# Half of the query, key and value projection moved into the attention, modulation on TensorE strips, and norm2 woven between first products

## The chip, the cores and the metric

The kernel runs on one NeuronCore of a Trainium2 chip. The metric is the device time of one execution in microseconds (us). The core has a matrix engine (TensorE, PE in the profile; PEld is its weight load), VectorE (DVE), ScalarE (ACT), GpSimd (POOL), and SyncE (SP), which mostly issues DMAs. Each engine works through its own queue in order.

## What is computed

The reference is one decoder layer on a sequence of 1024 positions, width 1024, in float32:

```python
mod = silu(c) @ ada_w + ada_b                        # six vectors of 1024
sh1, sc1, g1, sh2, sc2, g2 = split(mod, 6)
p = modulate(rmsnorm(x, norm1_g), sh1, sc1) @ w_in   # 1024 x 2048: q, k, v, u of 512 each
o_attn = stick_breaking(rmsnorm(q), rmsnorm(k), v)   # 8 heads of 64
o_ssm = s5(u, ...)                                   # 32 groups of 16 channels
x = x + g1 * (concat(rmsnorm(o_attn), rmsnorm(o_ssm)) @ w_out)
h = modulate(rmsnorm(x, norm2_g), sh2, sc2)
val, gate = split(causal_dwconv(h @ ffn_w_up), 2)    # 2 x 2816 channels
x = x + g2 * ((gelu(gate) * val) @ ffn_w_down)
```

## The kernel before, in words

Matrix products are made of three float32r products each: every operand is split into a rounded part and a rest (`hi`, `lo`), and hi·hi, hi·lo and lo·hi are summed in PSUM. ScalarE makes `hi` (`act_copy`, L160), VectorE or GpSimd the rest (`tt`, L61). Instructions are written out stage by stage, but the build orders each engine's queue by a simulated time line, so work of neighbouring stages is interleaved; `issue_after` and `high_priority` steer it.

The stages are these. **Norm 1 and u** (L152 to L238): for each of eight blocks k of 128 input channels, the shift and scale of the modulation are formed, the normalised x is transposed and modulated into `hhi[k]`, `hlo[k]`, and five of eight tiles of u are accumulated. The modulation vector is c times a 1024 x 256 slice of `ada_w`. For k = 0 it is 16 products with one column (L212). For the others VectorE makes it: a multiplication (L215) and seven multiply-adds (L217) into `ada_acc`, then two one-column products with `ones` sum over the partitions (L220). **State-space parameters** (L240 to L410) are a long string of small VectorE operations. **Query, key projection and state-space batches** (L591 to L625): `proj` (L549) makes 24 matmuls, 512 columns wide, for each of eight row tiles, for queries and for keys; then squares, sums per head (L606), a reciprocal root (`rsqrt`, L71), a scaling (L611), transposes (L615), the split `hl`, and DMAs from the ACT queue to the scratch tensor `qk_d`. Four `ssm_batch` (L429) stand among them. `ada_step` (L587) inserts pieces of `ada_back` (L560), which makes the other modulation vectors, apart from g2, by eight VectorE multiply-adds (L569) on 256 KB loads for each of six pieces of 512. **Values** (L640 to L648) go to `v_d`. 

**Attention** (`head`, L679) runs over eight heads, each in four groups of two query tiles: products z (L697, L698), two sigmoids (L701, L702), a running product on VectorE (the scan, L703), a product on GpSimd (L705), transposes (L710), the split `wh`, `wl` (L714, L715), and products with the values (L720, L721). The loads of the next head are issued with the first tile of the present one (L866). A generator of fillers (`fillers`, L801: the scaling of `w_out`, the statistics of the state-space output, and its half of the output projection) is advanced at fixed points (`marks`, L815), spread from 2% to 87.5% of the attention work. The last head runs its groups in falling order, with the statistics and output projection of finished groups behind them (`tail_stats`, `tail_proj`).

**Norm 2 and first products** (L994 to L1046): `norm2_x`, `norm2_t`, `norm2_s`, `norm2_4` make the operands of the up projection for four groups of 256 positions, the late half (groups 3 and 2) first. The up projection uses one level of Winograd's scheme, seven products of 12 matmuls per channel block m instead of eight, except m = 0, which takes eight direct ones; `first products` of m = 0 and two of m = 1 need only the late half. **Up** (L1128 to L1132): 21 further blocks, with convolution and gating (`conv`, L1090). `g2_rows` (L1051) makes the vector g2 by VectorE multiply-adds during blocks 6 to 9. **Down** (L1150 to L1190): for each half n of the output columns, 22 blocks with 24 matmuls each; the weights are multiplied by g2 on GpSimd (L1160) before they are split.

Of the kernel before, what the change touches and what calls it, by code (L numbers as in the profile page):

```python
# [35 lines left out]
def hybrid_layer_kernel(  # L36
# [53 lines left out]
    cols2_sb = const.tile([128, 194], F32, name="cols2_sb")  # L90
# [3 lines left out]
    gq_sb, gk_sb = cols2_sb[:, 192:193], cols2_sb[:, 193:194]  # L94

# [21 lines left out]
    x1_d = dram.tile([1024, 1024], F32, name="x1_d")  # L117
    x2_d = dram.tile([1024, 1024], F32, name="x2_d")
# [3 lines left out]

    A1 = const.tile([128, 8], F32, name="A1")
# [3 lines left out]
    g1row = const.tile([128, 1024], F32, name="g1row")  # L127
# [4 lines left out]
    hlo = [hp.tile([128, 1024], F32R, name=f"hlo{k}") for k in range(NK)]  # L132
    wp = alloc("w_in")
# [62 lines left out]
    def u_evac(m, hf):  # L196
        uF = wp.tile([128, 8, 64], F32, tag="uF", name="uF", bufs=3)
        act.activation(out=uF, in_=u_ps[m, hf].rearrange("p (c j) -> p j c", j=8), func=AF.Copy)
        sp.dma_start(out=u_d[m * 128:(m + 1) * 128, :, hf * 64:(hf + 1) * 64], in_=uF)

    for k in range(NK):
# [7 lines left out]
        if k == 0:  # L209
            for i in range(2):  # L210
                for r in range(8):
                    pe.matmul(mps[:, i:i + 1], lhsT=raw[:, r, i * 128:(i + 1) * 128], rhs=c_sb[:, r:r + 1], start=(r == 0), stop=(r == 7))  # L212
        else:
            acc = pn.tile([128, 256], F32, tag="ada_acc", name="ada_acc1")
            dve.tensor_scalar(out=acc, in0=raw[:, 0, :], scalar1=c_sb[:, 0:1], scalar2=None, op0=MUL)  # L215
            for r in range(1, 8):
                stt(acc, raw[:, r, :], c_sb[:, r:r + 1], acc, MUL, ADD)  # L217
            for i in range(2):
                cs_ = slice(i * 128, (i + 1) * 128)
                pe.matmul(mps[:, i:i + 1], lhsT=acc[:, cs_], rhs=ones[:, 0:1], start=True, stop=True)  # L220
        tt(dve, S1c[:, k:k + 1], mps[:, 0:1], sh1b[:, k:k + 1], ADD)
        stt(A1[:, k:k + 1], mps[:, 1:2], sc1b[:, k:k + 1], n1g_sb[:, k:k + 1], ADD, MUL)
# [312 lines left out]
    def load_wchunk(cix):  # L535
        his, los = [], []
        for k in range(NK):
            raw = wp.tile([128, 512], F32, tag="wraw", name="w_raw", bufs=4)
            with tc.issue_after(ada_dma[7].ins):
                sp.dma_start(out=raw, in_=w_qkv[cix, k])  # L540
# [241 lines left out]
    def run_all(gen):  # L782
        for _ in gen:
            pass
# [474 lines left out]
```

## Time and profile before

| | before |
|---|---|
| median of 3 runs | 1342.84 us (1341.87 to 1342.91) |
| the profiled execution's own time | 1337.98 us |
| its span, first to last instruction | 1336.2 us |
| PE, DVE, ACT, POOL busy | 1211.5, 1019.7, 594.0, 535.4 us |
| mean granted TensorE clock | 0.95 of full speed |

Busy is the time in which at least one instruction of the engine runs. The granted clock is 1.0 at 2.4 GHz and 0.5 at 1.2 GHz; a stretch between shows a mean of the two. A matmul's row gives its latency, not its pace: successive matmuls overlap, so the pace is the distance between two starts.

### The profile page before, as it was taken

The page shows a single profiled execution, that of the slowest core. Times are in us where ns is not written, and L with a number is a line of the kernel's source. Part 1 is how long each engine was busy: PE and PEld are TensorE (multiplying, and loading weights), DVE is VectorE, ACT ScalarE, POOL GpSimd, SP SyncE. Part 2 cuts the span into 40 slices and gives each one's busy share as a digit, 9 for nine tenths or more (in the row PEclk, how much of TensorE's full clock was granted, in tenths as well). Part 3 has the DMA queues.
Part 4 walks back from the last instruction along what each step waited for, and adds up shares of the span by engine and source line. Part 5 has one row for each costly group of instructions (what it writes and reads, how often), then busy time and mean ns, then how long its engine had stood idle before and what let it go on. Part 6 is the DMA issues. An engine that isn't in the chain of part 4 may idle for free.

```text
span 1336.2 us, 16685 instructions
## 1 busy us (share of the span) xinstructions
PE 1211.5 (91%) x5740; PEld 989.2 (74%) x5740; DVE 1019.7 (76%) x1531; ACT 594.0 (44%) x1006; POOL 535.4 (40%) x415
## 2 busy tenths in 40 slices
PE   5879989999769988679788999999999989999998
PEld 4667768777557776568567888788888878888887
DVE  6999988973887999996799678877777666554552
ACT  5431333331565676535554554445554543222320
POOL 4472451431762446810253553454435334222330
PEclk9989979989679999889889999999999999999999
DMA  8462445557943755041024223322222145447543
GB/s 342 159 143 55 131 136 148 152 152 241 252 111 99 215 175 173 16 142 79 17 87 134 81 88 102 103 95 79 79 93 81 56 157 196 145 145 239 174 142 111
DMA packets 125632, 177.83 MB, mean 133 GB/s; under 512 B 36454, under 2 KB 73958, under 8 KB 124524
## 3 DMA queue, kind: packets, MB, share of 16 engines
q1 hardware_dynamic: 105484, 156.85, 37.7%
q10 hardware_dynamic: 20064, 19.93, 4.5%
q8 instruction: 45, 0.74, 0.2%
q14 instruction: 39, 0.32, 0.1%
HBM read 134.67 MB, written 40.89 MB: 131 GB/s over the span
## 4 chain that ended last, share of the span: by engine, by line
PE 54%; DVE 28%; DMA 8%; issue 4%; ACT 3%; POOL 1%; SPq 1%; DVEq 0%; ACTq 0%; POOLq 0%
PE dnps L1175 6%; PE dnps L1176 6%; PE dnps L1174 6%; PE up_a L982 5%; PE up_a L984 5%; PE up_a L983 5%; DVE ada_acc L67 4%; DVE nb L703 3%; DMA ada_raw<-in_ada_r_dram 3%; PE up_c L982 2%; PE up_c L984 2%; PE up_c L983 2%; PE wops L776 2%; PE wops L777 2%; PE wops L778 2%
## 5 line engine op out<-in xcount | busy, mean ns | idle before, releaser
L61 POOL TENSOR_TENSOR S<-upraw 128x512 f32<-128x512 f32 x42 | 83.4, 1987 | 253.3 <-DVE uplo L61 173.2
L1175 PE MATMUL dnps<-wdlo,ahi 128*128 128x512 f32 x352 | 137.2, 390 | 0.8 <-DVE wdlo L61 0.8
L1174 PE MATMUL dnps<-wdhi,ahi 128*128 128x512 f32 x352 | 134.6, 390 | 3.4 <-ACT wdhi L160 3.4
L1176 PE MATMUL dnps<-wdhi,alo 128*128 128x512 f32 x352 | 137.1, 390 | 0.0
L61 DVE TENSOR_TENSOR uplo<-S,uphi 128x512 fp32r<-128x512 f32 x84 | 96.4, 1151 | 45.4 <-ACT uphi L160 44.2
L61 DVE TENSOR_TENSOR alo<-araw,ahi 128x1024 fp32r<-128x1024 f32 x44 | 61.9, 1407 | 87.7 <-ACT ahi L160 87.7
L61 POOL TENSOR_TENSOR sig<-sig,nb 128x127 f32<-128x127 f32 (+3 forms) x64 | 94.2, 1479 | 84.2 <-DVE nb L703 58.2
L67 DVE SCALAR_TENSOR_TENSOR cv<-up,cols_sb,cv 128x1023 f32<-128x1023 f32 x88 | 116.2, 1322 | 14.3 <-ACT cv L1095 13.2
L61 POOL TENSOR_TENSOR wdraw<-wdraw,g1row 128x512 f32<-128x512 f32 x44 | 69.4, 1581 | 140.7 <-DMA wdraw<-in_w_down_dram 136.3
L703 DVE TENSOR_TENSOR_SCAN nb<-nb 128x128 f32<-128x128 f32 (+3 forms) x64 | 108.4, 1708 | 2.3 <-ACT nb L701 2.0
L160 ACT ACTIVATE ahi<-araw 128x1024 fp32r<-128x1024 f32 x44 | 46.6, 1060 | 141.8 <-PE dnps L1175 119.3
L160 ACT ACTIVATE uphi<-S 128x512 fp32r<-128x512 f32 x84 | 52.7, 631 | 103.6 <-PE up_c L983 30.9
L67 DVE SCALAR_TENSOR_TENSOR ada_acc<-ada_raw,c_sb,ada_acc 128x256 f32<-128x256 f32 (+1 forms) x97 | 73.4, 771 | 25.6 <-DMA ada_raw<-in_ada_r_dram 23.7
L553 PE MATMUL qkvp<-w_hi,hhi 128*128 128x512 f32 x192 | 78.8, 412 | 3.8 <-DVE qssq L606 2.9
L554 PE MATMUL qkvp<-w_lo,hhi 128*128 128x512 f32 x192 | 78.4, 408 | 0.8 <-POOL w_lo L61 0.8
L1174 PEld LDWEIGHTS dnps<-wdhi,ahi 128*128 128x128 f32 x352 | 66.0, 188 | 17.6 <-ACT wdhi L160 3.8
L555 PE MATMUL qkvp<-w_hi,hlo 128*128 128x512 f32 x192 | 77.4, 403 | 0.0
L1175 PEld LDWEIGHTS dnps<-wdlo,ahi 128*128 128x128 f32 x352 | 66.1, 188 | 14.9 <-DVE wdlo L61 1.2
L1176 PEld LDWEIGHTS dnps<-wdhi,alo 128*128 128x128 f32 x352 | 66.1, 188 | 13.5
L160 ACT ACTIVATE uphi<-upraw 128x512 fp32r<-128x512 f32 x67 | 41.8, 629 | 64.5 <-PE up_a L983 26.7
L61 POOL TENSOR_TENSOR cv<-cv 128x1024 f32<-128x1024 f32 x22 | 54.5, 2475 | 34.6 <-ACT cv L1099 34.5
L1095 ACT ACTIVATE cv<-up,cols_sb 128x1024 f32<-128x1024 f32 x44 | 54.7, 1244 | 24.5 <-DVE up L61 23.8
(328 smaller groups left out, 3515.5 us busy)
## 6 DMA issues: line engine op xcount, KB each, us to landing
upraw<-in_w_up_dram SPq DMA_DIRECT2D x88, 256.0 KB, 2.6
araw<-a_d SPq DMA_DIRECT2D x44, 512.0 KB, 3.3
ada_raw<-in_ada_r_dram SPq DMA_DIRECT2D x48, 256.0 KB, 3.1
a_d<-cv ACTq DMA_DIRECT2D x22, 512.0 KB, 2.7
wdraw<-in_w_down_dram SPq DMA_DIRECT2D x44, 256.0 KB, 3.3
ada_raw<-in_ada_a_dram SPq DMA_DIRECT2D x8, 1024.0 KB, 9.4
qk_d<-hl ACTq DMA_DIRECT2D x32, 256.0 KB, 3.0
q<-qk_d SPq DMA_DIRECT2D x32, 256.0 KB, 6.0
```

What stands on the lines that cost most here:

```text
L61: eng.tensor_tensor(out=out, in0=a, in1=b, op=op)
L67: dve.scalar_tensor_tensor(out=out, in0=a, scalar=s, in1=b, op0=op0, op1=op1)
L160: act.activation(out=o, in_=i, func=AF.Copy)
L553: pe.matmul(o, lhsT=lh, rhs=his[k], start=(k == 0), stop=False)
L554: pe.matmul(o, lhsT=lh, rhs=los[k], start=False, stop=False)
L703: dve.tensor_tensor_scan(out=nb[:, 0:n][:, ::-1], data0=nb[:, 0:n][:, ::-1], data1=nb[:, 0:n][:, ::-1], initial=1.0, op0=MUL, op1=ALU.bypass)
L982: pe.matmul(ps, lhsT=hi[:, kt, :], rhs=rh, start=(first and kt == 0), stop=False, skip_group_check=True)
L983: pe.matmul(ps, lhsT=hi[:, kt, :], rhs=rl, start=False, stop=False, skip_group_check=True)
L984: pe.matmul(ps, lhsT=lo[:, kt, :], rhs=rh, start=False, stop=(kt == 3), skip_group_check=True)
L1174: pe.matmul(o[t], lhsT=hi[:, a], rhs=whi, start=(m == 0), stop=False)
L1175: pe.matmul(o[t], lhsT=hi[:, a], rhs=wlo, start=False, stop=False)
L1176: pe.matmul(o[t], lhsT=lo[:, a], rhs=whi, start=False, stop=(m == NM - 1))
```

## The change

- **Strips.** A vector c of 128 partitions is spread to 32 equal columns (`c32`). Each of the eight row blocks of a modulation slice is a float32 product with a stationary operand of 32 columns, written to one of four groups of 32 PSUM partitions (four column strips of the array). The strips hold partial sums; ScalarE copies them, and a product with a constant 1/32 (`mean32`) sums over the partitions. It replaces `ada_acc` in norm 1, in `ada_back` (which now makes g2 too, eight pieces, with two 1 MB loads each into one buffer) and `g2_rows`.
- **Projection in halves.** `load_wchunk` and `proj` take 256 output columns, four heads, at a time. Heads 0 to 3 are projected where all eight were. Heads 4 to 7 are projected by a generator `proj2` during the attention of heads 0 to 3. The fillers of before move to heads 4 to 7 and are placed at 50% to 87.5% of the attention work. At head 4 several pools are released and allocated, and the loads of head 4 are issued there, not during head 3.
- **Norm 2.** Blocks m = 0 and m = 1 both take eight direct products, and these are placed between the steps of norm 2 of groups 1 and 0.
- **Down.** g2 multiplies the output rather than the weights, the first operands are loaded at high priority, and buffers are divided in two pools by the parity of m. Raw up weights use four buffers and two of the attention's.

```diff
+    def strips(ps, raws):
+        for r in range(8):
+            j = r % 4
+            pe.matmul(ps[32 * j:32 * j + 32], lhsT=c32[:, r, :], rhs=raws[r], start=(r < 4), stop=(r >= 4))
...
+        strips(mps[:, 0:256], [raw[:, r, :] for r in range(8)])
+        acc = pn.tile([128, 256], F32, tag="ada_acc", name="ada_acc1")
+        act_copy(acc, mps[:, 0:256])
+        for i in range(2):
+            pe.matmul(mps[:, 256 + i:257 + i], lhsT=acc[:, i * 128:(i + 1) * 128], rhs=mean32[:, 0:1], start=True, stop=True)
...
+    def qk_pair(pl, nh, ps_o, ps_t, cix, hh, tq, w):
+        qk = pl.tile([128, 2, 4, 64], F32, tag="qk", name="qk", bufs=2)
...
+        for j in range(2):
+            proj(o[:, j * 256:(j + 1) * 256], tq * 2 + j, w)
+            if j == 0:
+                yield
+        qf = qk.rearrange("p j h d -> p (j h d)")
+        act.activation(out=qf, in_=o, func=AF.Copy)
+        act.activation(out=o, in_=o, func=AF.Square)
+        dve.tensor_reduce(out=ssq, in_=o.rearrange("p (h d) -> p h d", d=64), op=ADD, axis=AX.X)
+        yield
+        ts(dve, ssq, ssq, 1.0 / HD, EPS, MUL, ADD)
+        rsqrt(small, inv, ssq, 8)
+        yield
...
     def ada_back(ix):
...
+        for hf in range(2):
+            raw = stg.tile([128, 4, 512], F32, tag="adaq", name="ada_raw", bufs=1)
+            sp.dma_start(out=raw, in_=ada_r[ix, :, hf * 4:hf * 4 + 4])
+            if hf == 0:
+                yield
+            for i in range(4):
+                pe.matmul(ps[32 * i:32 * i + 32], lhsT=c32[:, hf * 4 + i, :], rhs=raw[:, i, :], start=(hf == 0), stop=(hf == 1))
+            if hf == 0:
+                yield
...
-    marks = [a + (b - a) * j / n for a, b, n in ((0.02, 0.14, 22), (0.14, 0.80, 24), (0.80, 0.875, 12)) for j in range(n)]
+    marks = [a + (b - a) * j / n for a, b, n in ((0.005, 0.46, 43), (0.50, 0.58, 22), (0.58, 0.82, 24), (0.82, 0.875, 12)) for j in range(n)]
...
+    def proj2():
+        for cix in range(3):
+            w = load_wchunk(pj, cix, 1, 4, 2)
+            yield
+            for tq in range(4):
+                if cix < 2:
+                    yield from qk_pair(pj, 1, psB_new, psB_new, cix, 1, tq, w)
+                else:
+                    yield from v_pair(pj, 1, psB_new, 1, tq, w)
...
+        if hd == NH // 2:
+            run_all(fill)
+            ap_.release()
+            pj.release()
+            hp.release()
...
+            fill = fillers()
+            stk = (head_load_qk(hd), head_load_v(hd))
...
     norm2_t(1, norm2_x(1))
-    norm2_s(1)
+    first_late(0, ("V", "a", 2), ("V", "b"), ("V", "a", 2), ("N", "b"))
+    up_early(1, ("A21", "A22"))
     with tc.high_priority():
         xn0 = norm2_x(0)
...
+    norm2_s(1)
     norm2_4(1)
     norm2_t(0, xn0)
+    first_late(1, ("N", "c"), ("V", "b"), ("N", "b"), ("V", "b"))
...
+    first_early(0)
     norm2_s(0)
+    first_early(1)
     norm2_4(0)
...
-        tt(pool, raw, raw, g2row[:, ns], MUL)
...
-            tt(dve, res, o[t], res, ADD)
+            t_ = dx.tile([128, 512], F32, tag="tmp", name="tmp", bufs=2)
+            tt(dve, t_, o[t], g2row[:, ns], MUL)
+            tt(dve, res, t_, res, ADD)
```

## Rows read from the trace of the kernel before

**Rows 1.** By stage: stretch, length, busy PE, PEld, DVE, ACT, POOL, clock, DMA, GB/s

```profile
0.00:337.00 337.00, 290.12 (x1472) 233.79 (x1472) 281.49 (x654) 113.50 (x184) 132.24 (x127) 0.93 0.56 165
337.00:443.00 106.00, 83.07 (x421) 66.53 (x422) 90.99 (x111) 65.80 (x141) 57.78 (x55) 0.80 0.58 160
443.00:577.00 134.00, 110.64 (x664) 92.73 (x663) 124.65 (x147) 86.81 (x203) 77.16 (x82) 0.93 0.45 137
577.00:650.00 73.00, 68.12 (x315) 55.76 (x314) 51.41 (x145) 35.35 (x66) 3.38 (x2) 0.97 0.29 101
650.00:680.00 30.00, 16.14 (x57) 10.75 (x56) 26.85 (x43) 16.25 (x32) 14.98 (x4) 0.72 0.05 18
680.00:1075.00 395.00, 390.28 (x1707) 320.90 (x1706) 308.97 (x324) 199.15 (x287) 175.45 (x101) 1.00 0.27 92
```

**Rows 2.** VectorE's groups from 0 to 337 us: count, busy, mean ns, idle before

```profile
L67 DVE SCALAR_TENSOR_TENSOR ada_acc<-ada_raw,c_sb,ada_acc 128x256 f32<-128x256 f32 (+1 forms) x97 | 73.4, 771 | 25.6 <-DMA ada_raw<-in_ada_r_dram 23.7 <-DMA o_d<-gt 1.8
...
L61 DVE TENSOR_TENSOR qk<-qk,qinv 128x512 f32<-128x512 f32 x16 | 12.4, 811 | 0.2
...
L606 DVE TENSOR_REDUCE qssq<-qkvp 128x8 f32<-128x512 f32 x16 | 10.8, 681 | 0.0
...
L67 DVE SCALAR_TENSOR_TENSOR rs_h<-qinv 128x16 f32<-128x16 f32 x24 | 8.7, 370 | 0.2
...
L67 DVE SCALAR_TENSOR_TENSOR hl<-qkT,gqk,hl 128x512 fp32r<-128x512 f32 x8 | 6.0, 748 | 3.0 <-ACT hl L618 3.0
```

**Rows 3.** TensorE in order of time: start us, us, at 512 columns

```profile
1149.95 0.39 PE L1174 MATMUL dnps<-wdhi,ahi 128*128 128x512 f32 x1
1150.18 0.39 PE L1175 MATMUL dnps<-wdlo,ahi 128*128 128x512 f32 x1
```

**Rows 4.** The same view at 256 columns, in the attention

```profile
480.23 0.28 PE L721 MATMUL ops<-wl,vsb 128*128 128x256 f32 x1
480.35 0.28 PE L720 MATMUL ops<-wh,vsb 128*128 128x256 f32 x1
```

**Rows 5.** The same view, float32 products, whole array

```profile
202.72 1.50 PE L524 MATMUL gps<-ys,G 128*128 128x128 f32 x12
204.06 1.02 PE L573 MATMUL adps<-ada_acc,ones 128*128 128x512 f32 x2
204.92 0.27 PE L615 MATMUL qkT<-ident,qk 128*128 128x128 f32 x1
```

**Rows 6.** The same view, float32 products on two column halves in turn

```profile
106.39 2.15 PE L490 MATMUL vps<-U,W 128*64 128x128 f32 x32
108.47 0.50 PE L553 MATMUL qkvp<-w_hi,hhi 128*128 128x512 f32 x1
```

**Rows 7.** DMA issues: count, size, us from issue to landing

```profile
ada_raw<-in_ada_a_dram SPq DMA_DIRECT2D x8, 1024.0 KB, 9.4
vsb<-v_d SPq DMA_DIRECT2D x8, 512.0 KB, 5.2
```

**Rows 8.** VectorE in order of time: two scans of 640 columns

```profile
521.13 1.48 DVE L703 TENSOR_TENSOR_SCAN nb<-nb 128x640 f32<-128x640 f32 x1
...
546.47 3.18 DVE L703 TENSOR_TENSOR_SCAN nb<-nb 128x640 f32<-128x640 f32 x1
```

**Rows 9.** GpSimd in order of time, beside the second scan

```profile
546.31 2.00 POOL L61 TENSOR_TENSOR sig<-sig,nb 128x1023 f32<-128x1023 f32 x1
```

**Rows 10.** TensorE's waits from 650 to 680 us: total, times, longest

```profile
PE tp L938 <- ACT h2f L939: 8.0, 5, 3.4
PE up_a L982 <- ACT uphi L160: 5.6, 1, 5.6
```

**Rows 11.** TensorE's waits from 680 to 1110 us

```profile
PE up_a L982 <- DVE up L61: 3.6, 3, 2.0
PE dnps L1174 <- ACT wdhi L160: 3.4, 1, 3.4
```

**Rows 12.** VectorE's groups from 680 to 860 us

```profile
L67 DVE SCALAR_TENSOR_TENSOR g2acc<-g2raw,c_sb,g2acc 128x256 f32<-128x256 f32 x28 | 22.4, 801 | 8.2 <-DMA g2raw<-in_ada_r_dram 8.0
```

More of the change, by code (lines that the diff above doesn't have):

```diff
@@ L208, in hybrid_layer_kernel @@
         mps = psU.tile([128, 512], F32, tag="mps", name="mps", bufs=1)
[L209 to L222, printed above, removed]
+        strips(mps[:, 0:256], [raw[:, r, :] for r in range(8)])
[3 more added lines that the diff above has]
+            pe.matmul(mps[:, 256 + i:257 + i], lhsT=acc[:, i * 128:(i + 1) * 128], rhs=mean32[:, 0:1], start=True, stop=True)
+        tt(dve, S1c[:, k:k + 1], mps[:, 256:257], sh1b[:, k:k + 1], ADD)
+        stt(A1[:, k:k + 1], mps[:, 257:258], sc1b[:, k:k + 1], n1g_sb[:, k:k + 1], ADD, MUL)
         hi = wp.tile([128, 512], F32R, tag="whi", name="wu_hi", bufs=8)
@@ L558, in hybrid_layer_kernel, with run_all @@
+    vlast = [None]
+    def run_all(gen):
+        for _ in gen:
+            pass
     TB, ZB, MB = 3, 2, 2
@@ L572, in ada_back @@
-        if kind == 0:
-            pe.matmul(ps, lhsT=ones, rhs=acc, start=True, stop=True)
-            act.activation(out=g1row[:, o:o + 512], in_=ps, func=AF.Copy)
+        if kind == 0:
+            row = g1row[:, o:o + 512]
+            sp.dma_start(out=row, in_=ada_br[ix:ix + 1, :].to_broadcast([128, 512]))
+        elif kind == 3:
+            row = wp.tile([128, 512], F32, tag="uF", name="g2", bufs=2)[0:1, :]
+            sp.dma_start(out=row, in_=ada_br[ix:ix + 1, :])
+        ps = psA.tile([128, 512], F32, tag="aux", name="adps")
@@ L575, in ada_back @@
+        act_copy(acc, ps)
+        yield
+        ps = psA.tile([128, 512], F32, tag="aux", name="adps")
+        if kind in (0, 3):
+            pe.matmul(ps, lhsT=mean32, rhs=acc, start=True, stop=True)
+            tt(dve, row, ps[0:row.shape[0]], row, ADD)
+            if kind == 3:
+                sp.dma_start(out=g2_d[ix - 6:ix - 5, :], in_=row)
         else:
             for j in range(4):
-                pe.matmul(ps[:, j:j + 1], lhsT=acc[:, j * 128:(j + 1) * 128], rhs=ones[:, 0:1], start=True, stop=True)
+                pe.matmul(ps[:, j:j + 1], lhsT=acc[:, j * 128:(j + 1) * 128], rhs=mean32[:, 0:1], start=True, stop=True)
@@ L626, in hybrid_layer_kernel @@
+            g = qk_pair(stg, 2, psA_o, psA_t, cix, 0, tq, w)
+            for _ in range(2):
+                ada_step(2)
+                next(g)
+            run_all(g)
     smb.release()
     sm.release()
-    xq = alloc("qkraw", side="right")
-    us = alloc("ffnmix", side="right")
     qp = alloc("qk", side="right")
-    xs = alloc("ossm", side="right")
+    op_ = alloc("oatt", side="right")
+    oT = op_.tile([128, NPAIR, 1024], F32, tag="oT", name="oT", bufs=1)
     def head_load_qk(hd):
@@ L1001, in hybrid_layer_kernel @@
     wo.release()
-    op_.release()
     xs.release()
```

304 lines of the change are left out of this document (148 added, 156 removed).

## The prediction, made before the changed kernel was run

> **What bounds the kernel now.** I read the busy time by stage first, then each stage's own groups and waits. The table shows three kinds of stage. Up to 337 us, where the first product of the attention starts, VectorE is busy for 281.5 of 337 us and TensorE for 290.1 at a mean clock of 0.93: both are near full, and VectorE has the added idle time [rows 1]. In the attention, 337 to 577 us, VectorE leads clearly: 91.0 of 106 us and 124.7 of 134, together 215.6 of 240, or 90%, while TensorE has 83.1 and 110.6 at clocks of 0.80 and 0.93 [rows 1]. From 680 us on TensorE is full (390.3 of 395 at clock 1.00), so nothing but less TensorE work or fewer stalls helps there. Between lies a hole: from 650 to 680 us TensorE is busy for 16.1 of 30 us at a clock of 0.72 [rows 1]. So the change takes VectorE work out of the first stage, puts TensorE work into a stage that VectorE bounds, and fills the hole.
>
> **The first stage (0 to 337 us).** VectorE loses the multiply-adds of the modulation: 97 of 0.77 us, 73.4 us busy, and with them a wait of 23.7 us for their loads [rows 2]. Seven opening multiplications go too; at the same length they are some 4 us. Half of the per-head work goes to the attention: of 16 scalings (0.811), 16 sums (0.681) and 16 splits (about 0.75) [rows 2] half is 18 us. The strings of small operations stay as many, since eight pairs of tiles remain. What comes (four row additions, some of a few columns) I set at 4 us. VectorE falls from 281.5 to about 190.
>
> TensorE: the pace is 0.23 us for 512 columns [rows 3] and 0.12 for 256 [rows 4]. The projection had 3 x 8 x 24 = 576 matmuls of the first kind, 131 us, and keeps 576 of the second, 69 us: 62 less. The strips add. A float32 product appears as two records; for 512 columns the two take 204.92 - 204.06 = 0.86 us [rows 5], so 0.43 for 256. On two halves of the array 32 records of 128 columns take 108.47 - 106.39 = 2.08 us, 0.065 each [rows 6], against (204.06 - 202.72)/12 = 0.112 on the whole array [rows 5]: two strips do overlap. Bounds for four products on four strips: one after the other 4 x 0.86 = 3.44 us, all together 0.86. I take all together, since two already run at 1.7 times the pace. In the 2.08 us the 16 pairs at 0.112 would take 1.8, so entering and leaving the strips costs up to 0.3 us; I charge 0.5. Then 16 groups of the six old and two new pieces cost 16 x 1.36 = 22 us, and eight blocks of norm 1, two rounds of 0.43 each, 8 x 1.36 = 11. The one-column products and the sums over partitions I set equal before and after. TensorE's busy time becomes 290 - 62 + 33 = 261.
>
> The Trainium skill, in "TensorEngine Tiling (Array Packing)", section Key Properties, says that changing the tiling mode drains TensorE; that speaks against 24 groups of strips between full-width matmuls. By that rule the sum would hold a drain twice per group, and the trace agrees that it is small: the 0.3 us above is all that rows 5 and 6 leave for it.
>
> VectorE's 190 us, with today's idle time less the 23.7, 337 - 281.5 - 23.7 = 32, end at 222. TensorE can't start before its first 1 MB load, 9.4 us [rows 7], so I let it start at 11: without a gap it ends at 272 with today's clock, at 261 x 0.93 + 11 = 254 with the clock at 1. If it keeps today's idle time (337 - 290 = 47 us) it ends at 308. I take 256, nearest to the full clock, since the groups that make it wait are VectorE's, and those shrink: the attention starts **81 us earlier**, between 29 and 115.
>
> A wait is added: `ada_back` has one buffer, so each of 16 loads of 1 MB starts when the last strips have read it, and behind a strip that waits stands every later matmul. Loads of this size landed in 9.4 us in the crowded first 50 us [rows 7]; one half of a pair's projection, 24 x 0.12 = 2.9 us, surely covers part of it. The queue order is simulated, so I assume projections are put in front of the strips, and price a failure as a rival.
>
> **The attention (337 to 577 us).** No instruction of the heads goes away. Added for heads 4 to 7: 576 matmuls of 0.12 us, 69 us, all beside heads 0 to 3; on VectorE eight pairs with a scaling, a sum, a split, 2.2 us, and a dozen small operations between 0.17 and 0.37 us [rows 2], 2 to 4.4 us, and four value splits: 36 to 55, I take 43. ScalarE gets copies of like number, and its queue 16 DMA issues; it was busy for 65.8 of 106 us [rows 1]. GpSimd gets 12 splits of the weights. A scan of 640 columns took 1.48 us alone and 3.18 beside a 2.00 us GpSimd product [rows 8, 9], so each of them may hold a scan up by about its own length, half of 2.00: up to 12 us, I take 5. VectorE then has 215.6 + 43 + 5 = 264 us, and at today's 90% this is 293.
>
> The Trainium skill, in "SBUF — State Buffer", section Who interferes with whom, says that a VectorE instruction with two SBUF inputs and a GpSimd instruction that reads SBUF exclude each other in full. By that alone the 12 us, not 5, would stand in the sum; the pair of scans agrees with full exclusion, but which meet is a matter of timing.
>
> At head 4 the loads of keys and values are no longer a head ahead; the value load lands in 5.2 us [rows 7], the keys and queries before it, and I charge 10 us for that start. So 303, **63 us longer**, between 40 (93% busy, no bubble) and 100 (heads 0 to 3, with three engines near full, at 75%). Heads 4 to 7 also get denser, as all old fillers are now theirs; that is within the sum, since the work is the same.
>
> **Norm 2 (577 to 680 us).** TensorE's hole is 13.9 us idle, of which 8.0 waits for ScalarE's transposed rows and 5.6 for operands after GpSimd's sums [rows 10], plus 16.1 x 0.28 = 4.5 us for the slow clock [rows 1]. The eight direct products give 11 us of matmuls between the steps, and m = 1 no longer waits for GpSimd. But it takes an eighth product, 12 x 0.23 = 2.7 us. **13 us shorter**, between 0 and 16; next late would be VectorE with 26.9 of 30 us.
>
> **Up and down.** VectorE loses 22.4 us of g2 and its wait of 8.0 [rows 12], which TensorE feels only through waits of 3.6 us [rows 11]: 3 shorter. The first down operands are loaded early: 3.4 us of waiting [rows 11], 3 shorter. GpSimd's weight product cost nothing, hidden by full TensorE. The last output tile has one VectorE operation more, as long as a 512-column scaling, about 0.7. Together **5 shorter**, between 0 and 8.
>
> **Sum.** -81 + 63 - 13 - 5 = -36 us against the profiled 1337.98, or 1302. The median of the runs lies 4.9 us above the profiled execution; I shift by that: 1342.8 - 36 = 1306.8, say **1307**. Its own range is 1280 to 1332.
>
> **Rivals.** *Strips stall on their loads (slower).* The queue puts the strips so that a 1 MB load is covered by only one half projection. For: one buffer, and VectorE already waited 23.7 us for loads of a quarter of this size [rows 2]. Against: those waits came mostly from three small buffers in turn. With landings of 6 us, between the 5.2 for half the size and the 9.4 of the crowd [rows 7], each costs 3.1, 16 make 50: 1357. It decides from 36/16 = 2.3 us per load. *The attention takes it all back.* Heads 0 to 3 have 69 us more TensorE and 43 more VectorE work; if they and the start of head 4 take the upper bound of 100, the time is 1344, no change. For: clock 0.80 and all engines rising together; against: in the stretch from 443 us VectorE was already busy for 93% beside the same fillers. *The strips do not overlap fully.* Two at a time adds 16 x 0.86 + 8 x 0.86 = 21 us: 1328; one at a time adds 62 us, 1369. Rows 6 speak against the latter; nothing shows four. *More than forecast.* The first stage ends at VectorE's bound of 222 and the attention takes 290: 34 + 13 less, 1260.
>
> **Chances.** Forecast 0.60, stalled loads 0.12, attention takes all 0.13, strips 0.10 (mostly two at a time), more 0.05. About 0.2% is what a measurement of this kernel can tell from no change. Slower: the stalls, half of the second rival and a little of the strips, 0.20; same: a part of the second, 0.05; faster 0.75. The range 1270 to 1350 leaves out the stalled loads and the best case, under 2 in 10.
>
> **What would show it.** The attention's first product near 256 us, with VectorE at about 190 us busy before it. No DMA named as releaser of strips for more than 2 us each. Groups of four strips 1 to 1.4 us apart, start to next full-width start. Heads 0 to 3 in 135 to 155 us with TensorE over 85% busy; VectorE some 264 us busy in the whole attention. Head 4 starting within 10 us of its loads. No stretch of 30 us with a clock under 0.9 between the attention and the up products. The forecast is wrong if the attention grows by more than the first stage shrinks, or if TensorE's waits before it name ada_raw.

## The result, and the profile after

The changed kernel takes 1490.49 us, median of 4 runs (1489.31 to 1491.63), against 1342.36 for the kernel before (4 runs, 1340.33 to 1342.91): a ratio of 1.1107, 95% interval 1.1087 to 1.1126. It is 148 us slower; I had forecast 36 us faster. The profiled execution after took 1491.63 us with a span of 1489.8, 153.6 more than the span before.

Four marks split both spans: the first product of the attention (z), the end of its last product with the values, the first down product, the end.

| stage | before, us | after, us | difference | forecast |
|---|---|---|---|---|
| up to the first z | 337.2 | 370.6 | +33.4 | -81 |
| attention | 241.7 | 368.6 | +126.9 | +63 |
| norm 2 and up | 512.7 | 506.4 | -6.3 | -13 and some of -5 |
| down | 244.6 | 244.2 | -0.4 | the rest of -5 |

The page of the changed kernel, parts 1 (busy time) and 6 (DMA issues, with us to landing):

```profile
PE 1281.8 (86%) x6552; PEld 1049.6 (70%) x6552; DVE 956.6 (64%) x1508; ACT 597.5 (40%) x1015; POOL 462.7 (31%) x362
...
ada_raw<-in_ada_r_dram SPq DMA_DIRECT2D x16, 1024.0 KB, 5.1
```

Its stages, with the columns of [rows 1]; they answer to those rows:

```profile
0.00:222.00 222.00, 186.77 (x1300) 156.30 (x1300) 152.12 (x467) 81.00 (x135) 86.66 (x89) 0.95 0.50 160
222.00:371.00 149.00, 81.05 (x374) 52.54 (x373) 32.22 (x64) 16.09 (x21) 15.79 (x19) 0.57 0.43 120
371.00:572.00 201.00, 154.86 (x1042) 139.66 (x1041) 122.16 (x220) 86.88 (x199) 69.94 (x75) 0.87 0.31 87
572.00:739.00 167.00, 128.43 (x650) 104.92 (x649) 131.04 (x164) 86.22 (x182) 75.24 (x73) 0.83 0.44 142
739.00:811.00 72.00, 58.74 (x252) 45.40 (x252) 46.42 (x132) 31.43 (x59) 8.87 (x5) 0.88 0.36 124
811.00:842.00 31.00, 28.95 (x126) 22.69 (x125) 27.56 (x48) 20.52 (x38) 0.00 (x0) 0.89 0.01 1
842.00:1240.00 398.00, 397.74 (x1738) 325.57 (x1737) 336.63 (x293) 203.89 (x293) 203.27 (x101) 1.00 0.24 81
```

VectorE lost the work that the change took from it: 152.1 + 32.2 = 184 us are busy before the attention, against 281.5 [rows 1]. The time did not follow. From 222 to 371 us no engine is full: TensorE is busy 81 of 149 us at a clock of 0.57, VectorE 32. In heads 0 to 3 (371 to 572 us; 123 us before) and 4 to 7 (572 to 739; 118 before) no engine is full either: VectorE is busy for 61% and 78% of them, where it had 90% [rows 1]. The hole of [rows 1] in norm 2, 16.1 of 30 us, is filled: 28.95 of 31 us.

**What the third row of the table hides.** The stage holds the end of the output projection, and that grew: from the last product with the values to the last projection product it is 54.8 us before (578.9 to 633.7) and 67.8 after (739.2 to 807.0), for nearly the same products. From there to the end of the span it is 702.5 before and 682.7 after, 19.8 shorter. TensorE's waits from 739 to 842 us, projection first, then what is left of the 8.0 and 5.6 us of [rows 10]:

```profile
PE wops L824 <- POOL wohi L177: 8.6, 2, 4.8
PE wops L825 <- POOL wolo L61: 2.6, 3, 1.2
...
PE tp L1011 <- ACT h2f L1012: 0.8, 1, 0.8
PE up_a L1055 <- ACT T1hi L174: 0.7, 1, 0.7
```

Three of the four weight tiles that this projection reads are split by GpSimd only now (737.6 to 757.8 us), one after another through one buffer; in the kernel before the last was under way at 578.7. In order of time, one of them:

```profile
741.11 3.43 DMA woraw<-in_w_out_dram
744.64 1.30 DVE woraw L67
...
746.01 1.05 POOL wohi L177
...
747.14 2.36 POOL wolo L61
```

**What fills 222 to 371 us.** First TensorE's waits there (total, times, longest), then the chain of waits that ends at the attention (start, us, what):

```profile
PE adps L640 <- DMA ada_raw<-in_ada_r_dram: 44.1, 9, 9.7
PE yps L522 <- DVE S L61: 7.8, 2, 5.7
```

```profile
322.20 1.91 PE adps L640 x8
...
324.13 5.01 DMA ada_raw<-in_ada_r_dram
...
329.18 1.58 PE adps L640 x8
...
341.02 7.74 DMA k<-qk_d
...
348.83 10.98 DMA ada_raw<-in_ada_r_dram
...
359.94 1.97 PE adps L640 x8
...
361.93 4.89 DMA ada_raw<-in_ada_r_dram
...
366.87 1.98 PE adps L640 x8
```

The loads land in 5.1 us by the page, sooner than those of [rows 7], and still it reads as strips, load, strips, load: with one buffer a load starts when the strips before it have run, and the next strips wait for it. As written, the code has a `yield` behind the first load of each piece but none between the second load and its strips, and all projections made ahead of the attention had ended at 227 us: ten of the 16 groups of strips came later, with only products of the state-space batches in front. One load was issued behind the key load in SP's queue and took 10.98 us. That queue stops as well: from 222 to 371 us it waits 32.0 us for strips to free the buffer, with loads of the batches and heads behind; no run separates this from TensorE's waits.

**The strips themselves** overlap as forecast. In order of time a group of four 512-column products (eight records) goes from 199.14 to 200.13 us, start to next full-width start, 0.99 us at full clock; one product on the whole array took 0.86 [rows 5]. Six of the 16 groups ran so; the ten behind 227 us took 1.6 to 1.9 us each, all but one wholly at half the clock. The row of TensorE's groups from 96 to 372 us (count, busy, mean ns, idle before) adds up to 25.4 us for all 16, where I had 22: a pace better than forecast and a clock that I had not forecast happen to give nearly that sum.

```profile
198.93 0.28 PE L564 MATMUL vp<-w_hi,hlo 128*128 128x256 f32 x1
199.14 1.06 PE L640 MATMUL adps<-ada_raw,c 128*32 128x512 f32 x8
200.13 0.38 PE L562 MATMUL vp<-w_hi,hhi 128*128 128x256 f32 x1
200.36 0.28 PE L563 MATMUL vp<-w_lo,hhi 128*128 128x256 f32 x1
```

```profile
L640 PE MATMUL adps<-ada_raw,c 128*32 128x512 f32 x128 | 25.4, 877 | 44.4 <-DMA ada_raw<-in_ada_r_dram 44.4
```

The Trainium skill, "TensorEngine Tiling (Array Packing)", section Key Properties, says that changing the tiling mode drains TensorE. The trace leaves room for it: 0.13 us in the group (0.99 - 0.86), 0.09 in front (0.21 from 198.93 to 199.14, against the pace of 0.12 [rows 4]) and 0.11 behind (0.23 from 200.13 to 200.36), together 0.33 us, near the 0.3 that the prediction allowed.

### The profile page after: what moved, and what is told of

It reads as the page before. It is cut to its first block, busy times and chain, and to the rows that moved or that the text cites. A ratio compares the mean times of both kernels' runs of the same rounds, so it can differ in the third digit from the quotient of the medians.

```text
span 1489.8 us, 18144 instructions
## 1 busy us (share of the span) xinstructions
PE 1281.8 (86%) x6552; PEld 1049.6 (70%) x6552; DVE 956.6 (64%) x1508; ACT 597.5 (40%) x1015; POOL 462.7 (31%) x362
## 3 DMA queue, kind: packets, MB, share of 16 engines
q1 hardware_dynamic: 100488, 157.38, 33.4%
## 4 chain that ended last, share of the span: by engine, by line
PE 66%; DVE 14%; DMA 9%; ACT 4%; POOL 3%; issue 2%; SPq 1%; ACTq 0%; DVEq 0%; POOLq 0%
PE dnps L1233 5%; PE dnps L1232 5%; PE dnps L1231 5%; PE up_a L1056 5%; PE up_a L1057 5%; PE up_a L1055 5%; DVE nb L751 3%; DMA ada_raw<-in_ada_r_dram 3%; PE up_c L1056 3%; PE up_c L1057 3%; PE up_c L1055 3%; PE qkp L563 2%; PE qkp L562 2%; PE qkp L564 2%; PE wops L824 2%
## 5 line engine op out<-in xcount | busy, mean ns | idle before, releaser
L67 DVE SCALAR_TENSOR_TENSOR cv<-up,cols_sb,cv 128x1023 f32<-128x1023 f32 x88 | 144.0, 1639 | 20.9 <-ACT cv L1157 18.8
L61 DVE TENSOR_TENSOR alo<-araw,ahi 128x1024 fp32r<-128x1024 f32 x44 | 55.5, 1262 | 122.5 <-ACT ahi L174 120.0
L61 POOL TENSOR_TENSOR S<-upraw 128x512 f32<-128x512 f32 x40 | 76.3, 1909 | 180.5 <-DVE uplo L61 89.7
L751 DVE TENSOR_TENSOR_SCAN nb<-nb 128x128 f32<-128x128 f32 (+3 forms) x64 | 99.7, 1571 | 3.4 <-ACT nb L749 3.2
L174 ACT ACTIVATE uphi<-S 128x512 fp32r<-128x512 f32 x80 | 49.8, 624 | 84.3 <-POOL S L61 67.8
L563 PE MATMUL qkp<-w_lo,hhi 128*128 128x256 f32 x256 | 76.6, 299 | 3.2 <-POOL w_lo L61 3.2
L562 PE MATMUL qkp<-w_hi,hhi 128*128 128x256 f32 x256 | 77.5, 303 | 0.0
L564 PE MATMUL qkp<-w_hi,hlo 128*128 128x256 f32 x256 | 76.5, 299 | 0.0
L61 DVE TENSOR_TENSOR uplo<-upraw,uphi 128x512 fp32r<-128x512 f32 x68 | 70.4, 1037 | 2.0 <-ACT uphi L174 1.9
L174 ACT ACTIVATE uphi<-upraw 128x512 fp32r<-128x512 f32 x68 | 42.9, 631 | 67.5 <-POOL cv L61 31.2
L824 PE MATMUL wops<-wohi,ohi 128*128 128x512 f32 x128 | 54.3, 431 | 13.4 <-POOL wohi L177 9.3
L768 PE MATMUL ops<-wh,vsb 128*128 128x256 f32 x160 | 51.0, 339 | 16.7 <-DVE oT L61 7.1
```

Source lines behind the costliest of these rows:

```text
L61: eng.tensor_tensor(out=out, in0=a, in1=b, op=op)
L67: dve.scalar_tensor_tensor(out=out, in0=a, scalar=s, in1=b, op0=op0, op1=op1)
L174: act.activation(out=o, in_=i, func=AF.Copy)
L562: pe.matmul(o, lhsT=lh, rhs=wh, start=(k == 0), stop=False)
L563: pe.matmul(o, lhsT=lh, rhs=wl, start=False, stop=False)
L751: dve.tensor_tensor_scan(out=nb[:, 0:n][:, ::-1], data0=nb[:, 0:n][:, ::-1], data1=nb[:, 0:n][:, ::-1], initial=1.0, op0=MUL, op1=ALU.bypass)
```

## Experiments

Kernels with one time ran once. The single runs of the kernel before spread over 1335 to 1346 us, so from one run a difference under some 10 us is not read without its trace.

### The second modulation: left out, put back on VectorE, moved, loaded in halves

**e1_no_back** leaves the second modulation's loads, strips and sums out (g1, sh2, sc2 and g2 are constants).

```diff
-    ada_gen = (q for ix in range(8) for q in ada_back(ix))
...
+    ada_gen = iter(())
```

> The changed kernel without its 16 loads of 1 MB, their strips and their sums (g1, sh2, sc2 and g2 are constants; the strips of norm 1 stay). Theory: after 222 us, when all projections are done, strips that wait for single-buffered 1 MB loads stand in TensorE's queue ahead of the last two state-space batches and of the attention; the chain of waits names these loads for about 75 us there. Without them the first product of the attention falls from 370.6 us to 285 to 300, the time to about 1405 to 1420. Rival: the four state-space batches, a serial chain through single buffers, bound the stage now that the projections no longer run beside them at a high clock; then the start falls by under 35 us, to 335 or later, and the time stays above 1455.

1378.76 us, 112 less than the changed kernel, more than expected; first z at 266.5 us. The state-space batches, which end at 321.0 in the changed kernel, end at 244.6. The rest of the stage:

```profile
222.00:266.00 44.00, 24.83 (x201) 22.11 (x200) 15.12 (x29) 12.68 (x17) 12.81 (x16) 0.82 0.59 157
```

So the batches did not bound the stage; they stood behind the second modulation's loads and strips. Without it the stage ends 71 us earlier than before; the forecast had 81, and that with 22 us of strips in it.

**e9_back_on_vector** puts only the second modulation back on VectorE.

```diff
-            raw = stg.tile([128, 4, 512], F32, tag="adaq", name="ada_raw", bufs=1)
-            sp.dma_start(out=raw, in_=ada_r[ix, :, hf * 4:hf * 4 + 4])
...
-                pe.matmul(ps[32 * i:32 * i + 32], lhsT=c32[:, hf * 4 + i, :], rhs=raw[:, i, :], start=(hf == 0), stop=(hf == 1))
...
+            raw = stg.tile([128, 512], F32, tag="adaq", name="ada_raw", bufs=3)
+            sp.dma_start(out=raw, in_=ada_r[ix, :, r])
...
+                stt(acc, raw, c_sb[:, r:r + 1], acc, MUL, ADD)
...
-                ada_step(2)
+                ada_step(4)
```

> The changed kernel with the second modulation alone put back on VectorE, as before the change (256 KB loads, three buffers in turn, one multiply-add per load; four pieces ahead of each half pair): everything else of the change stays. Theory that strips in TensorE's queue stop it at each load, while VectorE has time to wait: first product of the attention at 275 to 315 us instead of 371, attention and rest as in the changed kernel, time 1395 to 1435. Rival (the loads or the state-space batches bound the stage on whichever engine): first product at 340 to 370, time 1460 to 1490.

1434.78 us, 56 less; first z at 312.8. The theory holds, at the upper end. Against no second modulation at all (266.5) it costs 46 us on VectorE and 104 on strips. The same work costs over twice as much of this stage on strips, with these loads, as on VectorE.

**e7_early** asks for the strips earlier.

```diff
-                ada_step(2)
+                ada_step(4)
```

> The changed kernel with the strips of the second modulation asked for twice as often (four pieces instead of two ahead of each half pair of queries and keys), so that they end beside the first state-space batches and not behind the last. Theory that it is the place in the order that costs (loads between the late state-space batches, and an uncovered tail): first product of the attention at 290 to 320 us instead of 371, time 1410 to 1445. Rival (16 waits for a single-buffered load cost their 5 us in TensorE's queue wherever they stand): first product at 345 to 375, time 1465 to 1500.

1499.62 us, first z at 383.9: slower still. The strips end at 330.7 instead of 371.6, but the last state-space batch ends at 363.4 instead of 321.0, and TensorE has 79.9 of 162 us, at half the clock:

```profile
222.00:384.00 162.00, 79.88 (x349) 52.23 (x349) 34.51 (x64) 17.53 (x23) 21.86 (x25) 0.53 0.37 106
```

The theory that the place in the order costs falls: asked for earlier, the same loads delayed the state-space batches instead.

**e8_halves** keeps order and memory, with two 512 KB buffers and two loads ahead.

```diff
+        raw = stg.tile([128, 2, 512], F32, tag="adaq", name="ada_raw", bufs=2)
...
-            raw = stg.tile([128, 4, 512], F32, tag="adaq", name="ada_raw", bufs=1)
...
+            if n + 2 < 32:
+                ada_load(n + 2)
```

> The changed kernel with the same 1 MB of space as two buffers of 512 KB, each load issued as soon as its buffer is read, two ahead of the strips, at the same places in the order. Theory that the single buffer costs (a load starts only when the last strips have run, and TensorE's queue waits for all of it): first product of the attention at 300 to 330 us instead of 371, time 1420 to 1450. Rival (the loads stand behind others in SP's queue, and the state-space batches behind them): within 15 us of 371, time 1475 to 1495.

1470.0 us, first z at 354.3: between the two. TensorE's waits from 222 to 354 us fall from 44.1 to 23.0 us, and the start of the attention moves by 16:

```profile
PE adps L649 <- DMA ada_raw<-in_ada_r_dram: 23.0, 14, 6.3
```

So the single buffer is at least 16 of the 104 us that the second modulation costs on strips (e1), and neither theory holds in full: the chain of waits still goes from load to strips to load, six times 4.3 to 5.7 us and once 7.4. Two buffers of 1 MB were not tried.

### The three parts alone, in the kernel before

**e4_strips_norm1**: strips in norm 1 only.

```diff
-            dve.tensor_scalar(out=acc, in0=raw[:, 0, :], scalar1=c_sb[:, 0:1], scalar2=None, op0=MUL)
-            for r in range(1, 8):
-                stt(acc, raw[:, r, :], c_sb[:, r:r + 1], acc, MUL, ADD)
...
+        strips(mps[:, 0:256], [raw[:, r, :] for r in range(8)])
...
+        act_copy(acc, mps[:, 0:256])
```

> The kernel before with the strips in norm 1 alone. If the strips do what was forecast (four at once, about 1 us a group), VectorE loses some 30 us of multiply-adds before the state-space parameters, these end near 76 us instead of 101, and with a first stage bounded by VectorE the attention starts 15 to 25 us earlier: 1318 to 1328. Rival: the stage is bounded by the chain of four state-space batches and TensorE behind it; the earlier start is still passed on whole, but a part is lost where the projections are now late: 1328 to 1340. If the strips cost more than they save: above 1343.

1336.25 us, 5 runs (ratio 0.9951, 0.9929 to 0.9973), in the rival's range. The longest part of the state-space parameters ends at 71.2 instead of 101.0 us, but the first z stands at 340.9 against 337.2: of 30 us gained none reaches the attention, since TensorE was already busy for 214 of 233 us from 104 us on. The gain is 5 us by the timed runs; the two profiled spans differ by only 1.1 us, so I can't place it in a stage.

**e5_norm2_alone**: norm 2 between eight first products.

```diff
-    RAWS, OPS = 6, 7
+    RAWS, OPS, FIRST = 4, 8, 2
...
+    first_late(1, ("N", "c"), ("V", "b"), ("N", "b"), ("V", "b"))
...
+    first_early(0)
...
+    first_early(1)
```

> The kernel before with the third part of the change alone (norm 2 between eight first products of output blocks 0 and 1; g2 and the down operands as before). Forecast's step: 13 us shorter between the end of the attention and the full up products. The changed kernel showed 513 -> 506 us from the last output product of the attention to the first product of the last phase, so 4 to 10 us: a time of 1332 to 1338. Rival (the hole is refilled by another wait, VectorE's own 27 of 30 us): 1340 to 1343. If norm 2 costs: above 1345.

1335.07 us, 10 runs (0.996, 0.9936 to 0.9984). As expected, and half of the 13 us forecast. The hole is filled:

```profile
652.00:683.00 31.00, 29.32 (x137) 23.93 (x136) 27.48 (x44) 21.58 (x37) 8.66 (x4) 1.00 0.09 30
```

It still lasts 31 us, with VectorE at 27.5, and from the last product with the values to the first down product it is 506.1 us instead of 512.7. The waits of [rows 10] are gone, but others came. From the last projection product to the first down products, TensorE's waits of 22.6 us before add up to 15.4 here; the largest:

```profile
PE up_a L982 <- ACT up L160: 3.9, 3, 2.3
PE dnps L1180 <- ACT wdhi L160: 3.4, 1, 3.4
PE dnps L1181 <- DVE wdlo L61: 2.3, 1, 2.3
PE adps L1075 <- DVE g2acc L67: 2.3, 1, 2.3
```

In the changed kernel, where g2 is off VectorE here and the down operands come early, they add up to 2.3.

**e6_strips_small_norm2**: norm 1 and the second modulation on strips, each product on its own 256 KB load, three buffers; norm 2 as in e5. All heads are projected before the attention.

```diff
             raw = wp.tile([128, 512], F32, tag="uF", name="ada_raw", bufs=3)
             sp.dma_start(out=raw, in_=ada_r[ix, :, r])
-            stt(acc, raw, c_sb[:, r:r + 1], acc, MUL, ADD)
             yield
+            j = r % 4
+            pe.matmul(ps[32 * j:32 * j + 32], lhsT=c32[:, r, :], rhs=raw, start=(r < 4), stop=(r >= 4))
```

> The kernel before (all eight heads projected before the attention) with norm 1 and the second modulation on four strips, the second modulation's loads kept small (256 KB each, three buffers in turn), and norm 2 between first products. If strips and norm 2 are sound and only the large single-buffered loads and the moved projections cost: VectorE loses some 60 us before the attention but TensorE stays full there, so 10 to 20 us shorter in all, 1320 to 1335. Rival (strips at this place make TensorE wait for each 256 KB load, 48 of them): first product of the attention later than 345 us, time over 1345.

1356.14 us, 4 runs (1.011, 1.0077 to 1.0143), first z at 363.1: the rival. Its cause is only partly the waits, 13.2 us. TensorE's groups from 96 to 363 us:

```profile
L577 PE MATMUL adps<-ada_raw,c 128*32 128x512 f32 x96 | 41.7, 680 | 13.2 <-DMA ada_raw<-in_ada_r_dram 13.2
```

48 products, one per load, take 41.7 us, 0.87 each, as long as a whole-array product; in the changed kernel 64 in groups of four take 25.4. From its start to the next full-width start one product alone takes 0.98 us, about as long as a group of four:

```profile
188.16 1.05 PE L577 MATMUL adps<-ada_raw,c 128*32 128x512 f32 x2
189.14 0.50 PE L559 MATMUL qkvp<-w_lo,hhi 128*128 128x512 f32 x1
```

In e8, two together take 0.98 as well (198.75 to 199.73 us). So in this kernel the time goes per group, and the strips gain only where several stand together, for which their operands must be there at once.

**e11_strips_norm2**: the two gains, the edits of e4 and e5, together.

```diff
+        strips(mps[:, 0:256], [raw[:, r, :] for r in range(8)])
...
+    RAWS, OPS, FIRST = 4, 8, 2
```

> The kernel before with the two parts of the change that were faster by themselves: norm 1's modulation on strips, and norm 2 between first products; second modulation on VectorE and all eight heads projected before the attention, as before. If the two gains add (0.9951 and 0.996): ratio 0.989 to 0.993, 1327 to 1333 us, ahead of both kernels. Rival (norm 1's gain is only a shift that the wait for the projections takes back): 0.994 to 0.998.

1327.18 us, 6 runs (0.9902, 0.987 to 0.9935): the gains add. It is 1% ahead of the kernel before and far ahead of the changed one, with the second modulation on VectorE and all heads projected at their old place.

### Heads 0 to 3: the pairs

**e2_proj2_first** runs the projection of heads 4 to 7 to its end ahead of head 0's work.

```diff
-    fill = proj2()
+    run_all(proj2())
+    fill = iter(())
```

> The changed kernel with the projection of heads 4 to 7 run before head 0 instead of beside heads 0 to 3; nothing is left out. Theory: beside the heads it is a serial string (one pair every 20 us, of which 10 to 13 are a dozen small VectorE operations queued between scans), still unfinished when head 3 ends, and head 4 waits for all of it. Alone, a pair needs 13 us, as the last three did after head 3: about 8 x 13 + 4 x 6 + 10 = 140 us before head 0, then heads 0 to 3 take 75 to 90 us without it; first product of the attention to head 4 near 85, and the time within 25 us of the changed kernel, 1470 to 1515. Rival: heads 0 to 3 are long because engines are full; then they still take over 120 us without the filler, and the time is above 1540.

1511.45 us. The build put head 0's products beside the first pairs. With little else beside them (VectorE is busy for 61 of 169 us from 362 us on) the twelve pairs still take 156 us, 362.5 to 518.7. Heads 1 to 3 then take 66 us, 22 each, so full engines, the rival, are not what holds them. TensorE names the scaling in each of the eight query and key pairs:

```profile
PE qkT L588 <- DVE qk L61: 40.3, 8, 7.3
```

So a pair is a string: products, copy, sum, a dozen small VectorE operations, scaling, transposes; the next pair's products stand behind the transposes in TensorE's queue. **In the changed kernel** scans and splits of the heads come between its links. VectorE in order of time, from a pair's sum to its scaling:

```profile
400.26 0.69 DVE L578 TENSOR_REDUCE qssq<-qkp 128x8 f32<-128x512 f32 x1 [4.50 <-ACT qkp L577]
...
403.66 0.14 DVE L67 SCALAR_TENSOR_TENSOR rs_h<-qinv 128x8 f32<-128x8 f32 x1
403.72 1.22 DVE L751 TENSOR_TENSOR_SCAN nb<-nb 128x512 f32<-128x512 f32 x1
404.85 0.77 DVE L61 TENSOR_TENSOR rs_h<-rs_h,qssq 128x8 f32<-128x8 f32 x1
...
407.74 1.49 DVE L751 TENSOR_TENSOR_SCAN nb<-nb 128x640 f32<-128x640 f32 x1
...
409.53 1.17 DVE L61 TENSOR_TENSOR rs_h<-rs_h,qssq 128x8 f32<-128x8 f32 x1
...
411.16 0.67 DVE L61 TENSOR_TENSOR qk<-qk,qinv 128x512 f32<-128x512 f32 x1
```

10.9 us pass from the start of the sum to that of the scaling, for small operations that last 3.9 us per pair (31.2 us in all from 371 to 572 us, over eight). Over the eight pairs it is 9.6 us on average.

**e3_short_string** leaves out the three correction steps of the reciprocal root for heads 4 to 7 (the first estimate is used).

```diff
-        rsqrt(small, inv, ssq, 8)
+        rsqrt(small, inv, ssq, 8, 3 if hh == 0 else 0)
```

> The changed kernel with the reciprocal root of heads 4 to 7 cut from eleven small VectorE operations to two (its three Newton steps are left out there, so these heads are scaled roughly). It takes 8 x 9 operations of 0.17 us, 12 us of VectorE time, away. Theory of the serial string: each pair beside the heads loses 6 to 10 us of its 20, head 4 starts 35 to 65 us earlier than 201 us after the first product, and the time falls by 35 to 65 us, to 1425 to 1455. Rival (full engines): no more than the 12 us of work go, 1478 or later.

1446.99 us, 43.5 less. From sum to scaling it now takes 4.2 us on average, 5.4 less, eight times 43. Heads 0 to 3 take 157 us instead of 201. The first and the last of the eight sums, in the changed kernel and here (min/median/max ns, first and last start):

```profile
L578 DVE TENSOR_REDUCE qssq<-qkp x8: 691/692/693, 400.3 to 539.9; 128x8 f32<-128x512 f32 x8
```

```profile
L578 DVE TENSOR_REDUCE qssq<-qkp x8: 690/692/692, 403.2 to 495.5; 128x8 f32<-128x512 f32 x8
```

A pair every 19.9 us became one every 13.2. The VectorE time left out is 72 operations, 25 us in the changed kernel (not the 12 expected), and VectorE was busy for only 122 of the 201 us; the 43 us are those of the string. Head 4 can't start before its end, whatever VectorE's load is.

### Heads 4 to 7: the fillers

**e10_bare** leaves the state-space half of the output projection out of heads 4 to 7; x is copied instead.

```diff
-        yield from out_proj(osp, psB_new, oS, t, True, his, los, xt_, inv)
+        yield
```

(The four weight tiles and the statistics of that half are left out too, VectorE's part of them as well.)

> The changed kernel without the state-space half of the output projection beside heads 4 to 7 (its four weight tiles, the load of its rows with their statistics, and its 192 full-width products, some 44 us of TensorE): x is copied into the running sum through the same buffer instead. Theory that heads 4 to 7 are long (167 us against 118) since all these fillers now stand beside them: they fall to 115 to 130, time 1437 to 1455. Rival (the start of head 4 without keys and queries, and loads, keep them long): 145 to 165, time 1470 to 1490.

1427.57 us, 63 less, and heads 4 to 7 take 105 us instead of 167: more than expected. VectorE is back at 92 of 105 us:

```profile
569.00:674.00 105.00, 76.93 (x443) 62.84 (x441) 91.72 (x109) 69.18 (x166) 59.46 (x65) 0.84 0.59 186
```

These fillers hold 192 matmuls of 0.23 us, 44 us, and 39 us of VectorE's time (131.0 - 91.7), and cost 62 us: VectorE's 39, and 23 in which it idles (36 us of 167 against 13 of 105). Where they stand shows the idle part. From 654 to 715 us of the changed kernel, first the products of these tiles alone (14 of their 16 halves; PE, PEld, DVE, then clock), then all work in the same stretch:

```profile
654.00:715.00 61.00, 41.14 (x172) 31.82 (x172) 9.85 (x14) 1.00 0.51 181
```

```profile
654.00:715.00 61.00, 59.03 (x318) 49.28 (x316) 39.13 (x50) 28.84 (x56) 14.04 (x17) 1.00 0.51 181
```

TensorE is full, 59 of 61 us at full clock, and VectorE, which leads in the heads otherwise, falls to 39 of 61. Before, the same products lay between 372 and 515 us, with VectorE at 140 of 159 us (371 to 530).

**e12_x1_two** gives the rows of x and the weight rows a second buffer, **e13_spread** other due times:

```diff
-        xt_ = osp.tile([128, 1024], F32, tag="x1", name="x1", bufs=1)
+        xt_ = osp.tile([128, 1024], F32, tag="x1", name="x1", bufs=2)
...
```

> The changed kernel with two buffers instead of one for the rows of x and the weight rows of the output projection (the buffer that each of the eight state-space tiles fills, sums into and stores in turn, 7.6 us each between 654 and 715 us). Theory that this chain makes the fillers of heads 4 to 7 bunch: heads 4 to 7 fall from 167 to 125-150 us, time 1460 to 1480. Rival (the amount of filler work beside four heads instead of eight is what costs): 160 to 170, time 1484 to 1494.

```diff
-    marks = [... (0.50, 0.58, 22), (0.58, 0.82, 24), (0.82, 0.875, 12) ...]
+    marks = [... (0.50, 0.535, 22), (0.535, 0.83, 24), (0.83, 0.875, 12) ...]
```

> The changed kernel with other due times for the fillers of heads 4 to 7: weights and statistics due earlier (22 pieces in 3.5% of the attention instead of 8%), the eight state-space tiles over 29.5% of it instead of 24%. If the due times make them bunch: heads 4 to 7 fall by 15 us or more, time under 1476. Rival (the chain of one buffer, or the amount, sets their pace, whatever the due time): within 6 us of 1490.

e12: 1479.87 us, with heads 4 to 7 at 175. The tiles come 24 us sooner and no further apart (14 halves from 635 to 688 us). The time is gained behind the heads: from the last product with the values to the last projection product it is 45.4 us instead of 67.8, and TensorE names GpSimd's weight splits there no more (11.2 us in the changed kernel). So the single buffer of these weights costs the output projection some 22 us; with two, heads 4 to 7, where the weights are now made, grow by 8. e13: 1489.51 us, the 14 halves from 655 to 711. Neither the buffer nor the due times spread these tiles over the heads. Whether it is their amount beside four heads, or the order in which the build puts them, stays open; an order written by hand was not tried.

### Two losses undone at once

**e14_repaired** is e9 and e3 together; the correction steps of heads 4 to 7 are left out.

```diff
+        rsqrt(small, inv, ssq, 8, 3 if hh == 0 else 0)
...
+                stt(acc, raw, c_sb[:, r:r + 1], acc, MUL, ADD)
...
```

> The changed kernel with two things undone at once: second modulation on VectorE as in e9, and the square root of the moved pairs cut to its first estimate as in e3 (the three correction steps of heads 4 to 7 left out). One at a time they gave 56 and 43.5 us. If the losses lie in different stages they add: 1385 to 1397. Rival (one hides the other): 1400 to 1430.

1376.45 us, 114 less, even more than 56 + 43.5: the losses lie in different stages. Of the 14 more, some 7 are in the strings, which take 3.3 us here against 4.2 in e3, eight times; the rest is not accounted for. Heads 0 to 3 and 4 to 7:

```profile
314.00:463.00 149.00, 136.37 (x1020) 124.00 (x1020) 102.60 (x144) 84.44 (x196) 67.14 (x78) 0.97 0.42 117
463.00:625.00 162.00, 126.19 (x677) 103.65 (x675) 130.10 (x163) 88.78 (x188) 83.38 (x70) 0.88 0.44 147
```

Heads 0 to 3 take 149 us, inside the 135 to 155 of the prediction, with TensorE at 92%. Against the kernel before, by the spans: first stage 23 shorter, heads 0 to 3 25 longer, heads 4 to 7 43 longer, norm 2 and up 7 shorter. That is 38 slower still.

## Why the prediction was wrong

- **The failed step of the first stage** is "I assume projections are put in front of the strips". The projections had ended at 227 us, and ten of the 16 groups of strips came after them. My rival *strips stall on their loads* named this, with a threshold of 2.3 us per load; the row of L640 has 44.4 / 16 = 2.8. I gave it 0.12, and priced it too low: only the waits, 50 us. e1 shows 104 us up to the first z. Of these 44 are TensorE's waits and 39 the busy time of its strips and sums from 96 to 372 us (at half the clock a group takes 1.9 us); the other 21 I put down to what stood behind them, as e1's batches, 76 us earlier, suggest. I also took the wait of VectorE on its loads, 23.7 us, as a cost that goes. It had stopped only VectorE; the same wait in TensorE's queue stops projections and batches too.
- **VectorE's sums were right**: 184 us against 190 before the attention, 122 + 131 = 253 against 264 in it. The ends of the stages were not. Idle time was carried over as "today's", though the change makes new waits. That the strips' busy time came out too (25.4 against 22) is partly luck, as the rows above show.
- **The failed step of the attention** is the one that divides busy time by 90%; VectorE had 69%. "A dozen small operations" I priced at 2 to 4.4 us of VectorE time per pair. On a busy VectorE they are 9.6 us of delay in a string of about 20, and eight strings and the values must end before head 4. e3 took 43.5 us off by shortening this string alone. With the string cut and the second modulation on VectorE (e14), heads 0 to 3 fell into the forecast range. (The lower bound of 40 for the attention was a slip: 264 / 0.93 - 240 is 44.)
- **"That is within the sum, since the work is the same"** failed for heads 4 to 7, 49 us longer. VectorE is busy for 131 us there, against 112 in the last four heads before (460 to 579 us), and idle for 36 against 7. The first 19 us are work that came from the first four heads and was in my sum; the idle time was not. Most of it lies where TensorE runs eight tiles of the old fillers almost end to end.
- **Norm 2, up and down** came out, and luck has a part in it: 18 forecast, 19.8 from the last projection product to the end, and TensorE's waits from there to the first down products fell from 22.6 to 2.3 us. Norm 2 alone gave half of its 13 (e5), so the rest is the other parts, which I had priced at 5. They are not separated further. The 0.4 us of the row *down* do not count against them: the 3.4 us of [rows 11] lie just before its first product.
- **A term put at nothing** is the output projection behind the attention, 13 us longer: its weights go through one buffer, and with the fillers late they were made there. e12 shows it.
- The rival *attention takes it all back* allowed +100; it was +127 with the first stage longer as well. The two rivals were priced as alternatives, and came together. The range of 1270 to 1350 did not hold such a case.

## What to carry to other kernels

When work goes from an engine that may wait to one whose queue holds everybody's work, price each load behind the new instruction as a stop of that queue, and ask which instructions stand in front of it while the load runs; here VectorE had 97 us less to do before the attention, and the attention started 33 us later. When a chain of small dependent operations is moved beside a busy engine, count its links times the instructions that come between, not its busy time, above all if something must end before the next stage starts. Fillers are not the same work at half the space: look at what the pacing engine does while they run, and at what was prepared behind them. And split a stage where its parts can cancel: 13 us lost and 19 won stood in one row.

## What the hardware showed that I had not expected

A VectorE operation of 8 columns can last nearly as long as a GpSimd product. In the string above `rs_h` from 409.53 took 1.17 us, where the median of the 24 such operations is 0.166; it ends at 410.70, and GpSimd's product ends at 409.37 + 1.32 = 410.69. GpSimd in order of time:

```profile
409.37 1.32 POOL L61 TENSOR_TENSOR sig<-sig,nb 128x639 f32<-128x639 f32 x1 [1.71 <-DVE rs_h L67]
```

The Trainium skill, "SBUF — State Buffer", section Who interferes with whom, says that a VectorE instruction with two SBUF inputs contends with a GpSimd instruction that reads SBUF; this pair agrees. In the prediction I applied it to the scans and not to the small operations; this one is seven times as long as the median.

At full clock one float32 strip product of 512 columns (e6), two (e8) and four (the changed kernel) take the same time among full-width matmuls: 0.98, 0.98 and 0.99 us, start to next full-width start.
